# Own double buffer for the sums of w_down, and the convolution's swish split over two stages

## The chip, the cores and the metric

The kernel runs on one core of a Trainium2 chip. The metric is the device time of one execution in microseconds (us), lower is better. A core has a matrix engine (TensorE, in the profile PE, with its weight loads as PEld), VectorE (DVE), ScalarE (ACT), GpSimd (POOL) and SyncE (SP), which here issues the transfers between the main memory and the on-chip memory.

## The reference, cut to what matters

One layer of an encoder over 1024 tokens of width 1024, in float32:

```python
h = rmsnorm(x, norm_mix_pre)
# A) convolution branch: 512 channels
a = a_val * sigmoid(a_gate)                    # columns of h @ w_in
a = silu(layernorm(dwconv31(a), g, b))         # swish is the last step
# B) attention branch: 8 query heads, 2 key/value heads of 64
att = attention(rope(rmsnorm(q)), rope(rmsnorm(k)), v)
x = x + rmsnorm(concat([a, att]) @ w_out, norm_mix_post)
x = x + rmsnorm(cross_attention(rmsnorm(x), mem), norm_mem_post)
u = dwconv3(rmsnorm(x) @ w_up)                 # 2 x 2816 columns
x = x + rmsnorm((gelu(u_gate) * u_val) @ w_down, norm_ffn_post)
```

## The kernel before, in words

Every float32 product is made of three passes: both operands are split into a high part and a low part (`hi = round(v)`, `lo = v - hi`), and `hi*hi + hi*lo + lo*hi` are summed in the matrix accumulator (PSUM). A split is a copy on ScalarE and a subtraction on VectorE or GpSimd.

The stages, in the order of the profile's time: input projection of the convolution branch with its gate and its 31 taps (0 to about 240 us, the taps run on VectorE beside the memory projections); key, value and query projections with their norms and rotations (about 205 to 276); attention (276 to about 500, in 64 units of 128 queries and one head); output projection (480 to 590); cross-attention (590 to 790); the gated MLP's up-projection (780 to about 1250); the down-projection (1250 to the end).

Both MLP products use a recursive scheme with 7 products of blocks instead of 8. For the up-projection, the tokens are split into 4 blocks whose 7 combinations (`BO`, 14 tiles) stay on chip, and a loop over 22 blocks of 128 columns runs one round for each: 7 products of 12 matrix instructions (`product`), the first two in `up_first`, on a weight tile `wg`, the other five in `up_finish`, on combinations that `up_operands` makes of `wg` and `wv`. `up_finish` collects the products on VectorE (`add`, L819), applies the 3-tap convolution (L808, L809, L811), gelu and the multiplication (L842), and stores the result to `act_d` (L843).

The down-projection needs sums of blocks of `w_down`, which don't depend on the data. They are made inside the up-projection's loop, one half block a round: `down_load` fetches 4 blocks of 128x256 into a tile `wd` (L748), `down_sums` does four subtractions in place on VectorE (L754) and stores the tile to `T_d` in the main memory (L755). The down-projection loads them again much later (L892).

On-chip buffers come from pools of slots. A tile that is allocated when no slot is free waits until an older tile of the pool is used up. `raw` has 3 slots of 4 KB and holds the weights as they come from the main memory: in the MLP loop `wg`, `wv` and `wd`. `act` has 15 slots of 8 KB: in the MLP loop the 14 tiles of `BO`, then the tiles `acts` of the down-projection. `wp` has 7 slots of 8 KB: in the MLP loop the split operands `a1`, `a2`, `a3`, `a22` and the tiles `u`; in the query stage the split weights and `n4`, the normed convolution output; in attention the transposed weights `PH`, `PL` of the softmax. `rope` has 2 small slots, which also hold the broadcast reciprocals `rcb` of attention. PSUM has 4 single slots (`psB`) and 2 double ones (`psS`).

The order of the instructions on each engine's queue is set at compile time by a planner: it simulates a timeline and takes, for each engine that is free, the first instruction in program order whose operands and slots are ready. Each engine then runs its list in that order.

The swish of the convolution branch is `conv_apply(h)` for the two halves of the tokens: for each of 4 channel blocks 4 transposes on TensorE, the swish on ScalarE (L381), the high part by VectorE (L382), the low part by GpSimd (L383). Both halves run in attention's second unit (`u == 1`). ScalarE loads a table of functions when it goes from one nonlinear function to another (exp, swish, gelu). In attention the sums of exp are inverted once for two heads (L567), broadcast by GpSimd into `rcb` (L569), transposed on TensorE into `pRb` and multiplied to the output (L571).

Of the kernel before, what the change touches and what calls it, by code (L numbers as in the profile page):

```python
# [8 lines left out]
F32 = mybir.dt.float32  # L9
F32R = mybir.dt.float32r  # L10
AF = mybir.ActivationFunctionType
ALU = mybir.AluOpType
# [5 lines left out]
NF = 22  # L18
# [15 lines left out]
def encoder_block(ctx: ExitStack, tc: tile.TileContext, x, xT, mem, w_a, w_q, w_kv, w_mkv, w_mqT,  # L34
                  w_mo, w_out, w_up, w_down, cols, rows, g10, rope, out):
    nc = tc.nc
# [3 lines left out]
    small = ctx.enter_context(tc.tile_pool(name="small", bufs=4))  # L40
# [6 lines left out]
    def A(shape, name, dt=F32R):  # L47
        return ap.tile([128] + shape, dt, tag="a", name=name)

    def raw(name):  # L50
        return rawp.tile([128, 1024], F32, tag="raw", name=name)
# [4 lines left out]
    def psS(name):  # L56
        return psp.tile([128, 1024], F32, tag="S", name=name, bufs=2)

    def psB(name):
        return psp.tile([128, 512], F32, tag="B", name=name, bufs=4)  # L60

    def sm(n, name, bufs=2):
        return small.tile([128, n], F32, tag=name, name=name, bufs=bufs)

    def f(t):
        return t.bitcast(F32)
# [10 lines left out]
    def cc(i):  # L77
        return col[:, i:i + 1]

    def tr(out_, in_):  # L80
        nc.tensor.transpose(out=out_, in_=in_, identity=ident)  # L81
# [207 lines left out]
    with tc.high_priority(offset=-6000):  # L289
        for c in range(4):  # L290
            a, acc = a_t[c // 2][:, c % 2, :], accs[c % 2]
# [28 lines left out]
    for c in range(8):  # L320
        w = wsplit(w_mqT[c], f"wmq{c}")
        go = tmp("go")
        for g in range(2):
            p = psB("pg")
            for j in range(2):
                for dt_ in range(2):
                    e = (2 * g + j) * 2 + dt_
# [6 lines left out]
    for h in range(4):  # L334
        ws = [wsplit(w_mo[2 * h + j], f"wmo{2 * h + j}") for j in range(2)]
        for mt in range(2):
# [3 lines left out]
            for j in range(2):  # L340
                e = 2 * h + j
# [8 lines left out]
    mxh = [[A([4, 512], f"mxh{h}{g}") for g in range(2)] for h in range(2)]  # L350
    mxl = [[A([4, 512], f"mxl{h}{g}") for g in range(2)] for h in range(2)]
# [3 lines left out]
    def conv_stats(t):  # L355
        h, tt = t // 4, t % 4
        if tt == 0:
            n4[h] = wp.tile([128, 4, 512], F32, tag="w", name="n4")
        p = psS("pln")[:, :512]
        for c in range(4):  # L360
            tr(p[:, c * 128:c * 128 + 128], conv_out[c][:, t * 128:t * 128 + 128])
        n = n4[h][:, tt, :]
        nc.scalar.copy(out=n, in_=p)
        st = sm(6, "ssh2")
        mv = sm(2, "rh2")
        rs = sm(1, "rs")
        nc.vector.bn_stats(out=st, in_=n)
        nc.vector.bn_aggr(out=mv, in_=st)
        rsqrt(rs, mv[:, 1:2], 1, 1.0)
        nc.vector.tensor_scalar(out=n, in0=n, scalar1=mv[:, 0:1], scalar2=rs, op0=ALU.subtract, op1=ALU.mult)  # L370

    def conv_apply(h):
        for c in range(4):
            p = psB("plnT")
            s = n4[h][:, :, c * 128:c * 128 + 128]
            for tt in range(4):
                tr(p[:, tt * 128:tt * 128 + 128], s[:, tt, :])
            p3 = p.rearrange("p (t n) -> p t n", t=4)
            m3 = mxh[h][0][:, c, :].rearrange("p (t n) -> p t n", t=4)
            l3 = mxl[h][0][:, c, :].rearrange("p (t n) -> p t n", t=4)  # L380
            nc.scalar.activation(out=s, in_=p3, func=AF.Silu, scale=cc(C_LNG + c), bias=cc(C_LNB + c))  # L381
            nc.vector.tensor_copy(out=m3, in_=s)  # L382
            nc.gpsimd.tensor_tensor(out=l3, in0=s, in1=f(m3), op=ALU.subtract)  # L383

    b_ctx = tc.issue_after(c_end.ins)
# [57 lines left out]
    bufs, kpair = {}, [None]  # L443
# [50 lines left out]
    for i in range(16):  # L494
        if i < 16:
            (kv_proj if i < 8 else q_proj)(i % 8)
        if i >= 8:
            conv_stats(i - 8)
        upto = min(i - KV_LAG, 7) if i < 8 else min(7, 7 - KV_LAG + 2 * (i - 7))
        while nkv[0] <= upto:  # L500
            kv_transpose(nkv[0])
            nkv[0] += 1
        if i >= 8 + B_LAG:
            q_transpose(i - 8 - B_LAG)
# [4 lines left out]
    att_p, att_t, att_r, att_o = {}, {}, {}, {}  # L509

    def att_unit(u):
        hd, i, qp = (u // 2) % 8, u % 2, u // 16
        return hd, i, qp, qp // 2, (qp % 2) * 256
# [33 lines left out]
    def att_values(v):  # L547
        hd, _, qp, h, q0 = att_unit(2 * v)
        e, pr, kv = hd % 2, hd // 2, hd // 4
        hr = slice(64 * e, 64 * e + 64)  # L550
        PH, PL = att_t.pop(v)
        po = psB("po")[:, :256]
        nc.tensor.matmul(out=po, lhsT=V[:, kv, 0, :], rhs=PH[:, 0, :], start=True, stop=False)
        for k in range(8):
            nc.tensor.matmul(out=po[:64], lhsT=V[:, kv, k, 0:64], rhs=PL[:, k, :], start=False, stop=False)
        for k in range(1, 8):
            nc.tensor.matmul(out=po, lhsT=V[:, kv, k, :], rhs=PH[:, k, :], start=False, stop=k == 7)
        if hd == 0:
            att_o[qp] = tmp("o4")
        o = att_o[qp][:, pr * 256:pr * 256 + 256]  # L560
        nc.scalar.copy(out=o[hr], in_=po[64:128])
        nc.vector.tensor_tensor(out=o[hr], in0=po[:64], in1=o[hr], op=ALU.add)
        if e == 1:
            pb = psB("pRb")
            for i in range(2):
                rc = sm(2, "rc")
                nc.vector.reciprocal(out=rc, in_=att_r[qp, i][:, hd - 1:hd + 1])  # L567
                rcb = small.tile([128, 2, 64], F32, tag="rope", name="rcb", bufs=2)
                nc.gpsimd.tensor_copy(out=rcb, in_=rc.unsqueeze(2).to_broadcast([128, 2, 64]))  # L569
                tr(pb[:, i * 128:i * 128 + 128], rcb.rearrange("p a b -> p (a b)"))  # L570
            nc.vector.tensor_tensor(out=o, in0=o, in1=pb[:, :256], op=ALU.mult)  # L571
            qs_ = slice(q0, q0 + 256)
            nc.scalar.copy(out=mxh[h][1][:, pr, qs_], in_=o)
            nc.gpsimd.tensor_tensor(out=mxl[h][1][:, pr, qs_], in0=o, in1=f(mxh[h][1][:, pr, qs_]), op=ALU.subtract)

    LOOKAHEAD = 3
    for u in range(NU + LOOKAHEAD + 2):
        if u < NU:
            ex = att_scores(u)
            last_exp = ex  # L580
        w = u - LOOKAHEAD
        if 0 <= w < NU:
            att_transpose(w)
        v = w - 2
        if v >= 0 and v % 2 == 1:
            att_values(v // 2)
        if u in (2, 4, 6):
            q_transpose(8 - B_LAG + u // 2 - 1)
        if u == 1:
            conv_apply(0)  # L590
            conv_apply(1)


    def load8(src, name, nact):
# [25 lines left out]
    def transpose_split(src, dh, dl, tt):  # L620
        ts_ = slice(tt * 128, tt * 128 + 128)
        for g in range(2):
            p = psB("pTs")
            for k in range(4):
                tr(p[:, k * 128:k * 128 + 128], src[:, (4 * g + k) * 128:(4 * g + k + 1) * 128])
            p3 = p.rearrange("p (k t) -> p k t", k=4)
            nc.scalar.copy(out=dh[g][:, :, ts_], in_=p3)
            nc.vector.tensor_tensor(out=dl[g][:, :, ts_], in0=p3, in1=f(dh[g][:, :, ts_]), op=ALU.subtract)
# [11 lines left out]
    for t in range(8):  # L640
        h, tt = t // 4, t % 4
        y = psS("y1")
        tok_gemm(y, mxh[h], mxl[h], wo, tt)
        xr = gE[:, 1, :]
        nc.sync.dma_start(out=xr, in_=x[t])
        x1 = post_norm(y, gE[:, 0, :], xr, "x1")
        nc.sync.dma_start(out=x1_d[t], in_=x1)
        j = tmp("junk2")
        ss = sm(1, "ss")
        nc.scalar.activation(out=j, in_=x1, func=AF.Square, accum_out=ss)  # L650
        rsqrt(rs2[:, t:t + 1], ss, 1, 1.0 / D)
        transpose_split(x1, x1h[h], x1l[h], tt)
    rs2s = rstd1

    Gw = load8(G_d, "Gw", 1)
    Ph, Pl = halves("P")
    for t in range(8):
        h, tt = t // 4, t % 4
# [9 lines left out]
        sums, rc = sm(4, "rh8"), sm(4, "ssh2")  # L668
# [72 lines left out]

    T_d = drp.tile([NF // 2, 128, 4, 512], F32, name="T_d")

    wds = {}

    def down_load(fi):
        wds[fi] = raw("wd").rearrange("p (b n) -> p b n", b=4)
        nc.sync.dma_start(out=wds[fi], in_=w_down[fi // 2, :, :, fi % 2 * 256:fi % 2 * 256 + 256])  # L748

    def down_sums(fi):  # L750
        wd = wds.pop(fi)
        b11, b12, b22, b21 = [wd[:, b, :] for b in range(4)]
        for dst, in0, in1 in ((b11, b12, b11), (b12, b22, b12), (b22, b22, b11), (b21, b22, b21)):
            nc.vector.tensor_tensor(out=dst, in0=in0, in1=in1, op=ALU.subtract)  # L754
        nc.sync.dma_start(out=T_d[fi // 2, :, :, fi % 2 * 256:fi % 2 * 256 + 256], in_=wd)  # L755

    def a_split(dst, src, eng):
        nc.scalar.copy(out=dst[:, 0, :], in_=src)  # L758
# [96 lines left out]
    for fi in range(NF + 1):  # L855
        if fi < NF:
            if fi >= UP_PRE:
                up_first(fi)
            up_operands(fi)
            down_load(fi)  # L860
        if fi:
            up_finish(fi - 1)
        if fi < NF:
            down_sums(fi)

# [205 lines left out]
```

## Time and profile before

| | before |
|---|---|
| median of 3 runs | 1469.17 us (1468.13 to 1473.19) |
| profiled execution, its own time | 1470.58 us |
| its span, first to last instruction | 1468.5 us |
| TensorE busy, mean granted clock | 1391.3 us (95%), 0.982 |
| VectorE busy | 1083.4 us (74%) |
| ScalarE busy | 699.1 us (48%) |
| GpSimd busy | 522.3 us (36%) |
| moved by DMA | 170.08 MB |

The time around the span is 2.1 us in the profiled execution. A share of busy time is a mean over stages of different kinds; a stall of TensorE counts where it happens, and after some of them the granted clock is lower for a while.

### The profile page before, as it was taken

What the parts mean: (1) busy time and instruction counts of PE and PEld (TensorE: products, weight loads), DVE (VectorE), ACT (ScalarE), POOL (GpSimd) and SP (SyncE); (2) the same over time, 40 slices, a digit from 0 to 9 for tenths busy, and PEclk for the clock granted to TensorE, in tenths of its full rate; (3) what the DMA queues carried; (4) which work ended last, traced back from release to release, by engine and by line L of the source; (5) the groups of instructions that cost most, each with busy time, mean ns of one, the idle gap of its engine ahead of it and who ended that gap; (6) DMA issues with size and microseconds to landing.
All of it is one profiled execution on the core that took longest, in us unless ns stands there. A gap on an engine that the chain in (4) does not pass through costs nothing.

```text
span 1468.5 us, 18850 instructions
## 1 busy us (share of the span) xinstructions
PE 1391.3 (95%) x7020; PEld 1168.7 (80%) x7020; DVE 1083.4 (74%) x1464; ACT 699.1 (48%) x1192; POOL 522.3 (36%) x508
## 2 busy tenths in 40 slices
PE   7999999889999999999997899999998999999996
PEld 5889988678988888888885677777787777888885
DVE  7599898899999534335468777777777678986576
ACT  6325653678888524334344433343344333544452
POOL 6628877711111414002136533444455441000003
PEclk9999999999999999999998999999999999999999
DMA  6416760000000424113222443343343348622325
GB/s 209 136 50 207 254 240 13 20 1 1 1 2 29 165 94 142 46 43 130 86 86 75 155 143 129 125 135 129 131 129 113 130 143 308 251 90 90 108 86 208
DMA packets 74059, 170.08 MB, mean 116 GB/s; under 512 B 9712, under 2 KB 32496, under 8 KB 73968
## 3 DMA queue, kind: packets, MB, share of 16 engines
q1 hardware_dynamic: 73968, 168.88, 34.2%
q8 instruction: 55, 0.90, 0.3%
q14 instruction: 36, 0.29, 0.1%
HBM read 124.82 MB, written 44.04 MB: 115 GB/s over the span
## 4 chain that ended last, share of the span: by engine, by line
PE 48%; DVE 20%; DMA 12%; issue 8%; POOL 7%; ACT 4%; SPq 1%; DVEq 0%; POOLq 0%; ACTq 0%
DMA wd<-in_w_down_dram 5%; PE yd L91 4%; PE yd L92 4%; PE yd L90 4%; PE y L98 4%; PE y L100 4%; PE y L97 4%; DVE wd L754 3%; PE pPT L81 3%; DMA T_d<-wd 2%; PE sc L100 2%; PE sc L97 2%; PE sc L98 2%; DVE u L819 2%; PE sp L524 2%
## 5 line engine op out<-in xcount | busy, mean ns | idle before, releaser
L295 DVE SCALAR_TENSOR_TENSOR cacc<-conv,col,cacc 128x1009 f32<-128x1009 f32 (+14 forms) x120 | 145.8, 1274 | 4.7 <-ACT cacc L242 4.4
L85 POOL TENSOR_SCALAR rt<-ss 128x1 f32<-128x1 f32 (+1 forms) x43 | 14.9, 347 | 367.6 <-DVE ss L899 228.3
L91 PE MATMUL yd<-op 128*128 128x512 f32 x308 | 119.9, 390 | 0.5 <-DVE op L899 0.5
L92 PE MATMUL yd<-op 128*128 128x512 f32 x308 | 119.7, 389 | 0.0
L758 ACT CAST a<-s 128x512 fp32r<-128x512 f32 x88 | 51.5, 619 | 114.4 <-PE p L100 53.8
L754 DVE TENSOR_TENSOR wd<-wd 128x256 f32<-128x256 f32 x88 | 63.8, 725 | 55.0 <-DMA wd<-in_w_down_dram 40.8
L759 POOL TENSOR_TENSOR a<-wg,a 128x512 fp32r<-128x512 f32 x44 | 61.0, 1406 | 102.5 <-ACT a L758 102.1
L90 PE MATMUL yd<-op 128*128 128x512 f32 x308 | 97.1, 389 | 0.0
L909 ACT CAST op<-acts 128x512 fp32r<-128x512 f32 x77 | 47.9, 622 | 97.7 <-PE yd L92 86.6
L899 DVE TENSOR_TENSOR op<-acts,op 128x512 fp32r<-128x512 f32 x77 | 52.9, 687 | 45.5 <-ACT op L909 45.4
L545 DVE TENSOR_TENSOR PL<-pPT,PH 128x512 fp32r<-128x512 f32 x128 | 82.7, 680 | 5.0 <-ACT PH L544 4.6
L527 DVE TENSOR_REDUCE nm<-sp 128x1 f32<-128x1024 f32 x64 | 78.0, 1219 | 3.2 <-PE sp L525 2.2
L809 DVE SCALAR_TENSOR_TENSOR c<-u,col,c 128x1023 f32<-128x1023 f32 x44 | 56.5, 1284 | 28.9 <-ACT c L808 28.9
L530 ACT ACTIVATE P<-sp,nm 128x1024 f32<-128x1024 f32 x64 | 72.2, 1129 | 8.8 <-PE pPT L81 5.1
L544 ACT CAST PH<-pPT 128x512 fp32r<-128x512 f32 x128 | 69.2, 593 | 13.5 <-PE pPT L81 12.8
L81 PE MATMUL pPT<-ident,P 128*128 128x128 f32 x512 | 69.5, 276 | 2.4 <-DVE PL L545 1.0
L759 DVE TENSOR_TENSOR a<-s,a 128x512 fp32r<-128x512 f32 x88 | 59.4, 694 | 12.3 <-ACT a L758 12.3
L91 PEld LDWEIGHTS yd<-op 128*128 128x128 f32 x308 | 57.8, 188 | 13.2 <-DVE op L899 1.3
L81 PEld LDWEIGHTS pPT<-ident,P 128*128 128x128 f32 x512 | 59.7, 142 | 10.6 <-DVE PL L545 3.1
L90 PEld LDWEIGHTS yd<-op 128*128 128x128 f32 x308 | 57.8, 188 | 12.0
L92 PEld LDWEIGHTS yd<-op 128*128 128x128 f32 x308 | 57.8, 188 | 12.0
L808 ACT ACTIVATE c<-u,col 128x1024 f32<-128x1024 f32 x44 | 53.2, 1209 | 26.9 <-DVE u L819 25.9
(341 smaller groups left out, 4401.0 us busy)
## 6 DMA issues: line engine op xcount, KB each, us to landing
wg<-in_w_up_dram SPq DMA_DIRECT2D x22, 512.0 KB, 3.7
wv<-in_w_up_dram SPq DMA_DIRECT2D x22, 512.0 KB, 4.3
wd<-in_w_down_dram SPq DMA_DIRECT2D x22, 512.0 KB, 3.9
T_d<-wd SPq DMA_DIRECT2D x22, 512.0 KB, 3.2
act_d<-u SPq DMA_DIRECT2D x22, 512.0 KB, 5.1
acts<-act_d SPq DMA_DIRECT2D x22, 512.0 KB, 8.3
st<-T_d SPq DMA_DIRECT2D x20, 512.0 KB, 3.7
wmkv_r<-in_w_mkv_dram SPq DMA_DIRECT2D x16, 512.0 KB, 4.2
```

What stands on the lines that cost most here:

```text
L81: nc.tensor.transpose(out=out_, in_=in_, identity=ident)
L90: nc.tensor.matmul(out=ps, lhsT=sh, rhs=mh, start=first, stop=False)
L91: nc.tensor.matmul(out=ps, lhsT=sh, rhs=ml, start=False, stop=False)
L92: nc.tensor.matmul(out=ps, lhsT=sl, rhs=mh, start=False, stop=last)
L97: nc.tensor.matmul(out=p, lhsT=sh, rhs=mh, start=first, stop=False)
L98: nc.tensor.matmul(out=p, lhsT=sh, rhs=ml, start=False, stop=False)
L100: ins = nc.tensor.matmul(out=p, lhsT=sl, rhs=mh, start=False, stop=last)
L295: nc.vector.scalar_tensor_tensor(out=acc[:, t0:t1_], in0=a[:, t0 + o:t1_ + o], scalar=cc(C_DW + c * 31 + j), in1=acc[:, t0:t1_], op0=ALU.m ...
L527: nc.vector.reduce_max(out=nm, in_=sp, axis=AX.X, negate=True)
L545: nc.vector.tensor_tensor(out=PL[dst], in0=p3, in1=f(PH[dst]), op=ALU.subtract)
L754: nc.vector.tensor_tensor(out=dst, in0=in0, in1=in1, op=ALU.subtract)
L759: eng.tensor_tensor(out=dst[:, 1, :], in0=src, in1=f(dst[:, 0, :]), op=ALU.subtract)
```

## The change

Three edits. First, `wd` leaves the `raw` slots: a tile `wd_b` of two halves is taken once from the `act` pool, a round's load goes into one half a round ahead of its sums, and its store is issued a round behind them. Second, `conv_apply(0)` moves from attention's start into the query stage (`i == 13` of 16), `conv_apply(1)` behind the first token block of the output projection, and the high part goes from VectorE to GpSimd in both. Third, attention inverts its sums for four heads at a time: half as many reciprocals (of 4 columns), as many broadcasts and transposes, half as many multiplications, copies and subtractions of twice the width.

```diff
@@ conv_apply
             nc.scalar.activation(out=s, in_=p3, func=AF.Silu, scale=cc(C_LNG + c), bias=cc(C_LNB + c))
-            nc.vector.tensor_copy(out=m3, in_=s)
+            nc.gpsimd.tensor_copy(out=m3, in_=s)
             nc.gpsimd.tensor_tensor(out=l3, in0=s, in1=f(m3), op=ALU.subtract)
@@ query stage
         if i >= 8:
             conv_stats(i - 8)
+        if i == 13:
+            conv_apply(0)
@@ att_values
-        if e == 1:
+        if hd % 4 == 3:
             pb = psB("pRb")
             for i in range(2):
-                rc = sm(2, "rc")
-                nc.vector.reciprocal(out=rc, in_=att_r[qp, i][:, hd - 1:hd + 1])
-                rcb = small.tile([128, 2, 64], F32, tag="rope", name="rcb", bufs=2)
-                nc.gpsimd.tensor_copy(out=rcb, in_=rc.unsqueeze(2).to_broadcast([128, 2, 64]))
-                tr(pb[:, i * 128:i * 128 + 128], rcb.rearrange("p a b -> p (a b)"))
-            nc.vector.tensor_tensor(out=o, in0=o, in1=pb[:, :256], op=ALU.mult)
-            qs_ = slice(q0, q0 + 256)
-            nc.scalar.copy(out=mxh[h][1][:, pr, qs_], in_=o)
-            nc.gpsimd.tensor_tensor(out=mxl[h][1][:, pr, qs_], in0=o, in1=f(mxh[h][1][:, pr, qs_]), op=ALU.subtract)
+                rc = sm(4, "rc")
+                nc.vector.reciprocal(out=rc, in_=att_r[qp, i][:, hd - 3:hd + 1])
+                for c in range(2):
+                    rcb = small.tile([128, 2, 64], F32, tag="rope", name="rcb", bufs=2)
+                    nc.gpsimd.tensor_copy(out=rcb, in_=rc[:, 2 * c:2 * c + 2].unsqueeze(2).to_broadcast([128, 2, 64]))
+                    tr(pb[:, c * 256 + i * 128:c * 256 + i * 128 + 128], rcb.rearrange("p a b -> p (a b)"))
+            o2 = att_o[qp][:, pr * 256 - 256:pr * 256 + 256]
+            nc.vector.tensor_tensor(out=o2, in0=o2, in1=pb, op=ALU.mult)
+            o3 = o2.rearrange("p (c q) -> p c q", c=2)
+            dst = (slice(None), slice(pr - 1, pr + 1), slice(q0, q0 + 256))
+            nc.scalar.copy(out=mxh[h][1][dst], in_=o3)
+            nc.gpsimd.tensor_tensor(out=mxl[h][1][dst], in0=o3, in1=f(mxh[h][1][dst]), op=ALU.subtract)
@@ attention loop
-        if u == 1:
-            conv_apply(0)
-            conv_apply(1)
@@ output projection
         transpose_split(x1, x1h[h], x1l[h], tt)
+        if t == 0:
+            conv_apply(1)
@@ MLP
-    wds = {}
+    wd_b = A([2, 4, 256], "wd", F32)
+
+    def down_slice(dr, fi):
+        return dr[fi // 2, :, :, fi % 2 * 256:fi % 2 * 256 + 256]
 
     def down_load(fi):
-        wds[fi] = raw("wd").rearrange("p (b n) -> p b n", b=4)
-        nc.sync.dma_start(out=wds[fi], in_=w_down[fi // 2, :, :, fi % 2 * 256:fi % 2 * 256 + 256])
+        nc.sync.dma_start(out=wd_b[:, fi % 2], in_=down_slice(w_down, fi))
 
     def down_sums(fi):
-        wd = wds.pop(fi)
-        b11, b12, b22, b21 = [wd[:, b, :] for b in range(4)]
+        b11, b12, b22, b21 = [wd_b[:, fi % 2, b, :] for b in range(4)]
         for dst, in0, in1 in ((b11, b12, b11), (b12, b22, b12), (b22, b22, b11), (b21, b22, b21)):
             nc.vector.tensor_tensor(out=dst, in0=in0, in1=in1, op=ALU.subtract)
-        nc.sync.dma_start(out=T_d[fi // 2, :, :, fi % 2 * 256:fi % 2 * 256 + 256], in_=wd)
+
+    def down_store(fi):
+        nc.sync.dma_start(out=down_slice(T_d, fi), in_=wd_b[:, fi % 2])
@@ MLP loop
             up_operands(fi)
-            down_load(fi)
-        if fi:
+        if fi == 0:
+            down_load(0)
+        else:
+            down_store(fi - 1)
             up_finish(fi - 1)
         if fi < NF:
             down_sums(fi)
+        if fi + 1 < NF:
+            down_load(fi + 1)
```

## Rows read from the trace of the kernel before

**Rows 1.** Windows by stage: TensorE, weight loads, VectorE, ScalarE, GpSimd, granted clock, DMA
```profile
276.00:320.00 44.00, 32.88 (x189) 26.83 (x188) 41.05 (x58) 35.56 (x58) 19.17 (x23) 0.88 0.00 1
353.00:376.00 23.00, 22.75 (x165) 20.49 (x164) 21.70 (x35) 19.21 (x39) 2.50 (x6) 1.00 0.01 2
500.00:600.00 100.00, 100.00 (x475) 83.47 (x474) 40.41 (x43) 36.86 (x65) 27.30 (x45) 1.00 0.37 125
799.00:1233.00 434.00, 405.96 (x1727) 329.23 (x1727) 326.12 (x420) 163.88 (x227) 194.11 (x146) 0.98 0.42 139
```

**Rows 2.** TensorE's waits, 800 to 1200 us: releaser, total, times, longest
```profile
PE p L97 <- DVE q L819: 16.7, 8, 3.0
PE p L97 <- ACT a L758: 4.4, 2, 2.9
PE p L97 <- DVE u L819: 3.6, 2, 3.1
```

**Rows 3.** Line L842, once a round: duration min/median/max, first and last start
```profile
L842 DVE TENSOR_TENSOR u<-u,c x22: 1206/1210/1222, 822.6 to 1266.2; 128x1024 f32<-128x1024 f32 x22
```

**Rows 4.** TensorE in order of time: the product `t2` of two rounds
```profile
1054.31 0.39 PE L97 MATMUL p<-t2h,a 128*128 128x512 f32 x1
...
1073.35 0.39 PE L97 MATMUL p<-t2h,a 128*128 128x512 f32 x1
```

**Rows 5.** One stall in order of time, SyncE, VectorE, then TensorE
```profile
999.80 0.57 SPq L748 DMA_DIRECT2D wd<-in_w_down_dram  x1
...
1000.50 1.29 DVE L809 SCALAR_TENSOR_TENSOR c<-u,col,c 128x1023 f32<-128x1023 f32 x1 [1.28 <-ACT c L808]
1003.57 1.54 DVE L754 TENSOR_TENSOR wd<-wd 128x256 f32<-128x256 f32 x1 [1.78 <-DMA wd<-in_w_down_dram]
1005.03 0.68 DVE L819 TENSOR_TENSOR q<-p,q 128x512 f32<-128x512 f32 x1
...
1005.85 0.47 PE L97 MATMUL p<-b21h,a 128*128 128x512 f32 x1 [3.00 <-DVE q L819]
```

**Rows 6.** Waits of VectorE, SyncE's queue and ScalarE, 800 to 1200 us
```profile
DVE wd L754 <- DMA wd<-in_w_down_dram: 40.8, 15, 5.0
DVE c L809 <- ACT c L808: 25.6, 25, 1.3
...
SPq L617 <- DMA T_d<-wd: 48.8, 18, 4.4
...
ACT a L758 <- DMA act_d<-u: 77.7, 16, 8.2
```

**Rows 7.** Lines L754, L382 and L569: duration ns min/median/max
```profile
L754 DVE TENSOR_TENSOR wd<-wd x88: 406/424/1539, 798.8 to 1215.8; 128x256 f32<-128x256 f32 x88
...
L382 DVE CAST mxh<-n x8: 415/952/1508, 284.7 to 294.7; 128x512 fp32r<-128x512 f32 x8
...
L569 POOL COPY rcb<-rc x32: 288/293/1293, 298.9 to 481.4; 128x128 f32<-128x128 f32 x32
```

**Rows 8.** A window without a wait of TensorE
```profile
1052.00:1087.00 35.00, 35.00 (x155) 28.95 (x154) 26.24 (x34) 13.63 (x20) 15.33 (x12) 0.99 0.50 165
```

**Rows 9.** TensorE's longest wait, 276 to 320 us, and ScalarE's groups, 276 to 300
```profile
PE sp L524 <- ACT P L530: 7.4, 3, 4.0
...
L381 ACT ACTIVATE n<-plnT,col 128x512 f32<-128x512 f32 x8 | 5.7, 782 | 0.1
L381 ACT ACT_TABLE_LOAD x2 | 2.6, 1283 | 0.0
L530 ACT ACT_TABLE_LOAD x2 | 2.6, 1283 | 2.1 <-DVE nm L527 2.1
```

**Rows 10.** A window at the end of the query stage; eight transposes in the chain of waits
```profile
270.00:276.00 6.00, 6.00 (x32) 5.06 (x31) 5.42 (x10) 3.14 (x6) 4.77 (x9) 1.00 0.28 98
...
708.44 0.87 PE pTs L81 x8
```

**Rows 11.** The page's DMA issues, the stores of the sums: count, KB each, median us to landing
```profile
T_d<-wd SPq DMA_DIRECT2D x22, 512.0 KB, 3.2
```

## The prediction

> **What bounds the kernel now.** I read the windows by stage first. In the output projection TensorE is busy for all of 100 us, in attention for 22.75 of 23.00 us; in the MLP loop it is busy for 406.0 of 434.0 us at a granted clock of 0.98, and over the 44 us in which attention starts for 32.9 at a clock of 0.88 [rows 1]. So there are two places where TensorE loses time, and the reader should see that no other engine is full there, save VectorE at attention's start (41.05 of 44).
>
> How much is lost in the loop follows from its period. The multiplication that ends a round starts 22 times between 822.6 and 1266.2 us, which is 443.6 / 21 = 21.12 us a round [rows 3]. Where TensorE doesn't wait, the same product of two rounds in a row starts 1073.35 - 1054.31 = 19.04 us apart [rows 4]. The excess is 2.08 us a round, 43.7 us in 21 rounds.
>
> Who takes it: TensorE waits 16.7 + 3.6 us for VectorE's sums of products and 4.4 us for ScalarE's splits between 800 and 1200 us [rows 2]. The stall of 3.00 us before 1005.85 shows why VectorE is late: it has a subtraction of the w_down sums at the head of its list, and its tile was only issued at 999.80 and is released at 1003.57; the collection of a product (`q`) runs behind it at 1005.03, and TensorE goes on 0.82 us later [rows 5]. Over the 400 us VectorE waits 40.8 us for `wd`, 15 times. The queue shows the ring behind it: the next weight tile's load waits 18 times, 48.8 us in all, for the store of the sums to land [rows 6]. Three tiles a round pass through three slots, and the slowest to return is `wd`.
>
> **Part 1, the double buffer.** It removes `wd` from the ring of three, and puts the load a round ahead of the sums. Loads, sums and stores are the same 22 each; nothing is added on any engine. VectorE's 40.8 us of waiting then have no cause in the load.
>
> What TensorE gets of this: without the wait the subtraction starts when L809 ends, at 1000.50 + 1.29 = 1001.79; it takes 0.42 us alone, or 1.54 as here [rows 5, 7], so `q` starts at 1002.2 to 1003.3 instead of 1005.03 and TensorE goes on at 1003.0 to 1004.1 instead of 1005.85. That gives back 1.7 to 2.85 of the 3.00 us; I take 2.3, or 77%. TensorE is idle 434.0 - 406.0 = 28.0 us over the loop [rows 1]; less the 4.4 us for ScalarE, 23.6 us are VectorE's, of which 23%, 5.4 us, stay. Of the 4.4 us I keep half, 2.2, because that ring is eased too (two tiles a round in three slots), but the loop's start is also crowded by other splits. The clock, 0.98 over 434 us, is worth some 9 us; it falls after waits, so it stays in their proportion: 9 x 7.6 / 28.0 = 2.4. Idle time and clock explain 37 of the 43.7; of the other 6.7 I keep half, 3.4. So 5.4 + 2.2 + 2.4 + 3.4 = 13.4 us stay and **30 us** go. Bounds: 0 (another wait ends at the same time) and 43.7.
>
> Can the others follow at 19.04 us? In a stretch of 35 us without a wait VectorE is busy for 26.24, which is 14.3 us a round, ScalarE for 7.4 and GpSimd for 8.3 [rows 8]. VectorE also waits 25.6 us in some 19 rounds, 1.3 us a round, for ScalarE's start of the convolution [rows 6]. That makes 15.6, so 3.4 us are free.
>
> What is late next: the tile `u` returns to `wp` when `act_d` has landed, and ScalarE waits 77.7 us for that, 16 times [rows 6]; TensorE waited for ScalarE only in the 4.4 us above. The slot of `wd_b` is the 15th of `act`, which only the raw blocks leave free when the last of the 14 operands is made; the first load can so come late by one landing, some 3.8 us by [rows 5], once. I put it at 0: VectorE is collecting the first products meanwhile; without that cover it costs the 3.8. The tiles `acts` lose that slot until the loop's end, when four operand tiles of the finished first products come free.
>
> **Part 2, the swish.** Attention's start loses 44.0 - 32.9 = 11.1 us of TensorE, and 7.4 of them are three waits for a slot that exp must free [rows 1, 9]. ScalarE is held there by 8 swishes (5.7 us) and four table loads (2 x 2.6 us) that change between swish and exp [rows 9]. Afterwards one load for exp is left there, and the swishes are gone: 5.7 + 3 x 1.28 = 9.5 us less. VectorE loses 8 casts of 0.95 us, 7.6 us [rows 7], from its 41.05. It was the fuller one, so it sets the bound: 41.05 - 7.6 = 33.4, and with its old idle time of 2.95 the stretch is 36.4 instead of 44: 7.6 us gained. The swishes' 32 transposes move to where TensorE is full [rows 1, 10]: 4 x 0.87 = 3.5 us. Net **4 us**.
>
> The moved work's own price: GpSimd gets 4 casts and 4 subtractions near the end of the query stage, where it is busy for 4.77 of 6 us [rows 10]. A cast of 128x512 on GpSimd isn't in the trace; the nearest rows are 0.29 us for a 128x128 broadcast there and 0.42 for the cast on VectorE [rows 7], so 0.4 to 4 x 0.29 = 1.2 us; I take 1.0. Queued behind them are the last queries' norms, for which VectorE and attention's last transposes of the queries wait; they are needed units later, so 0, and 4 x 1.2 = 4.7 us if that cover is gone. In the output projection GpSimd is busy for 27 of 100 us and ScalarE for 37 [rows 1], and the second half's result is read four blocks later: 0, or one table load of 1.3 us. `n4` of the second half now holds a `wp` slot through attention: six are left, three pairs of `PH`, `PL`, and six for the output weights; 0, or one more 128x1024 copy and subtraction in the open, an estimated 2.4 us from L842's 1.21 [rows 3]. Bounds of part 2: from 8 gained to 8 lost.
>
> **Part 3, the reciprocals.** VectorE saves some of its small instructions, but TensorE is busy for 22.75 of 23.00 us in that stretch [rows 1], so of 8 groups at most 8 x 0.25 = 2 us are to be had. Against it, four broadcasts now pass through two slots at a time; the second two wait for TensorE's first transposes. If TensorE has nothing else then, a group costs two broadcasts, 0.6 us, at the most the longest one seen, 1.29 [rows 7]: 5 to 10 us. Other units' transposes are ready in the steady state, so I take 0.
>
> **Sum.** 30 + 4 = 34 us off the profiled execution's own 1470.6 gives 1436.6. That execution lies 1.4 us above the median of 1469.2, so the forecast is **1435**.
>
> **A rule against it.** The subtractions of L754 take 0.42 us in the median and up to 1.54, the casts of L382 0.42 to 1.51 [rows 7]. If each of the four of a round met GpSimd, VectorE would need 14.3 + 4 x (1.54 - 0.42) = 18.8 us, with its 1.3 us of waits 20.1: it would be the bound, the gain 21 x (21.12 - 20.1) = 21 us, and with part 2 the time 1444. The Trainium skill, "SBUF — State Buffer", "Who interferes with whom", says that a VectorE instruction with two on-chip inputs and a GpSimd one that reads the on-chip memory lock each other out for a whole instruction; the spread of these rows agrees.
>
> **Rivals.**
> - *The slots of `wp` take over.* ScalarE's 77.7 us of waiting for `act_d` become TensorE's wait every other round. For it: 16 waits of up to 8.2 us. Against: hardly any reached TensorE. At half of the 30 us the time is 1450.
> - *VectorE is the bound* by the lock above: 1444. Against: the median of 0.42 says that most don't meet.
> - *No change.* The collections are late for other reasons and VectorE idles elsewhere: only part 2 moves, 1465 to 1469. Against: the order of [rows 5].
> - *Slower: SyncE's queue.* The load of round fi + 1 must wait until the store of fi - 1 has left the same half. If that store is issued just ahead, the queue stands for its landing of 3.2 us [rows 11] and 0.6 us of issue [rows 5], and the weight loads behind it are late. From 2.08 us a round on it costs more than is gained; at 3.8 us a round takes 22.8, 36 us more over 21, and the time is 1501. For it: 18 such waits now. Against: the sums are done a round before, so the store can have landed long ago.
>
> **Chances.** Forecast 0.62, `wp` 0.17, VectorE 0.05, all of the 43.7 us and more 0.04, no change 0.05, slower 0.07. A measurement tells 0.3% (4.4 us) from nothing; faster is 0.88, same 0.05, slower 0.07. The range reaches from 1418 (43.7 + 8 gained) to 1462 (a quarter of the 30 us gained, part 2 at 0), which takes in the first two rivals and leaves out the last two.
>
> **What would show it.** Right: no wait of L754 for `in_w_down`; L842 every 19.2 to 19.9 us; TensorE's idle time in the loop under 12 us; the granted clock there at 0.99; two table loads fewer between 276 and 300 us. Part 2 right: L382 on GpSimd in the query stage and behind 500 us, attention's first 20 units some 7 us shorter. Wrong: a new releaser of TensorE in the loop, a weight load that waits for `T_d`, a query stage longer than before by more than 2 us, or transposes of `pRb` with waits for GpSimd.

## The result, and the profile after

The kernel after takes 1455.9 us (median of 6 runs, 1452.9 to 1460.8) beside 1470.4 for the kernel before on the same chip: a ratio of 0.990, 95% interval 0.988 to 0.992. It is 14.5 us faster where 34 were forecast. The profiled execution, 1460.75 us, is the slowest of the six. One of the six executions of the kernel before took 4892.3 us; without it their median is 1470.3.

The windows by stage of the kernel after (columns as in [rows 1]), with the loop cut in two:

```profile
276.00:320.00 44.00, 35.96 (x197) 29.76 (x196) 37.41 (x53) 28.63 (x50) 16.73 (x25) 0.92 0.04 13
799.00:990.00 191.00, 170.51 (x697) 135.79 (x696) 158.06 (x223) 67.36 (x95) 84.19 (x63) 0.95 0.60 198
990.00:1220.00 230.00, 230.00 (x1017) 190.44 (x1015) 167.49 (x197) 95.48 (x131) 111.52 (x84) 1.00 0.29 94
799.00:1233.00 434.00, 413.51 (x1769) 337.00 (x1768) 336.99 (x435) 168.43 (x232) 195.71 (x146) 0.98 0.45 148
```

In the second half of the loop TensorE is never idle. The whole of the 20.5 us of idle TensorE lies in the first 191 us, at a granted clock of 0.95 and with the DMA engines busy for 0.60 of the time. The lines say why (the subtractions of the sums, formerly L754, the multiplication that ends a round, formerly L842, and the cast L382):

```profile
L759 DVE TENSOR_TENSOR wd<-wd x88: 408/418/1522, 807.4 to 969.2; 128x256 f32<-128x256 f32 x88
```
```profile
L849 DVE TENSOR_TENSOR u<-u,c x22: 1207/1211/1222, 822.9 to 1255.1; 128x1024 f32<-128x1024 f32 x22
```
```profile
L382 POOL CAST mxh<-n x8: 607/613/617, 274.1 to 520.7; 128x512 fp32r<-128x512 f32 x8
```

All 88 subtractions now run between 807.4 and 969.2 us, where they had been spread to 1215.8 [rows 7]; the rounds after that have none. A load "a round ahead" in program order may go as soon as its half is free, and the planner let it: loads, sums and stores of 22 rounds were pressed into the first 8 or so. A round takes (1255.1 - 822.9) / 21 = 20.58 us instead of 21.12 [rows 3], so the loop gained 443.6 - 432.2 = 11.4 us.

The waits between 800 and 1200 us, which answer to [rows 2, 6]:

```profile
DVE wd L759 <- DMA wd<-in_w_down_dram: 19.4, 12, 3.5
...
PE p L97 <- ACT a L765: 13.3, 4, 5.0
...
PE p L97 <- DVE u L826: 3.4, 2, 1.8
PE p L97 <- DVE q L826: 2.7, 5, 0.7
```
```profile
SPq L754 <- DMA T_d<-wd: 51.0, 18, 5.5
...
SPq L762 <- DVE wd L759: 35.6, 13, 8.9
```

TensorE's wait for VectorE's collections fell from 20.3 to 6.1 us, but its wait for ScalarE's splits rose from 4.4 to 13.3. SyncE's queue now stands both for the store to land before a load (51.0 us) and for the subtractions before a store (35.6). One stall of the kernel after, in order of time:

```profile
964.12 0.33 SPq L850 DMA_DIRECT2D act_d<-u  x1
...
969.69 0.53 SPq L762 DMA_DIRECT2D T_d<-wd  x1
969.91 1.14 ACT L765 CAST a<-wv 128x512 fp32r<-128x512 f32 x2 [8.48 <-DMA act_d<-u]
...
972.75 0.50 PE L97 MATMUL p<-b11h,a 128*128 128x512 f32 x1 [4.36 <-ACT a L765]
```

ScalarE waits 8.48 us for a slot that the store of `act_d` holds, and that store, issued at 964.12, is put down as what ended the wait at 969.91. TensorE waits 4.36 us for the next tile's split, which ScalarE makes behind this one. Two more of TensorE's four waits for ScalarE are of this form: 4.96 us before 881.56 and 3.06 before 927.41, behind waits of ScalarE of 10.84 and 7.14 us for `act_d`. The three make 12.4 of the 13.3 us.

### The profile page after: what moved, and what is told of

Same layout as the page of the kernel before. It is cut to its first block, busy times and chain, and to the rows that moved or that the text cites. A ratio compares the mean times of both kernels' runs of the same rounds, so it can differ in the third digit from the quotient of the medians.

```text
span 1459.0 us, 18771 instructions
## 1 busy us (share of the span) xinstructions
PE 1388.8 (95%) x7020; PEld 1170.3 (80%) x7020; DVE 1074.9 (74%) x1432; ACT 699.6 (48%) x1184; POOL 523.2 (36%) x508
## 4 chain that ended last, share of the span: by engine, by line
PE 71%; DVE 11%; DMA 9%; issue 3%; ACT 3%; POOL 3%; SPq 0%; POOLq 0%; DVEq 0%; ACTq 0%
PE p L97 6%; PE p L98 6%; PE p L100 6%; PE yd L90 5%; PE yd L91 5%; PE yd L92 5%; PE y L98 4%; PE y L100 4%; PE y L97 4%; DMA wd<-in_w_down_dram 3%; PE pPT L81 3%; DVE wd L759 2%; PE sc L100 2%; PE sc L97 2%; PE sc L98 2%
## 5 line engine op out<-in xcount | busy, mean ns | idle before, releaser
L766 POOL TENSOR_TENSOR a<-wg,a 128x512 fp32r<-128x512 f32 x44 | 62.8, 1448 | 82.4 <-ACT a L765 82.4
L766 DVE TENSOR_TENSOR a<-s,a 128x512 fp32r<-128x512 f32 x88 | 66.7, 772 | 17.2 <-ACT a L765 17.2
L546 ACT CAST PH<-pPT 128x512 fp32r<-128x512 f32 x128 | 69.5, 594 | 13.3 <-PE pPT L81 12.8
L759 DVE TENSOR_TENSOR wd<-wd 128x256 f32<-128x256 f32 x88 | 56.8, 654 | 20.0 <-DMA wd<-in_w_down_dram 19.4
L91 PEld LDWEIGHTS yd<-op 128*128 128x128 f32 x308 | 57.8, 188 | 12.4 <-DVE op L910 0.4
L766 POOL TENSOR_TENSOR a<-wv,a 128x512 fp32r<-128x512 f32 x22 | 33.3, 1533 | 96.0 <-ACT a L765 96.0
```

What stands on the lines that cost most here:

```text
L91: nc.tensor.matmul(out=ps, lhsT=sh, rhs=ml, start=False, stop=False)
L766: eng.tensor_tensor(out=dst[:, 1, :], in0=src, in1=f(dst[:, 0, :]), op=ALU.subtract)
```

## The experiments

"Paced" below is the kernel after with this edit: the load of round fi + 1 is issued no earlier than `act_st[fi - 1]`, the store of `act_d` of round fi - 1. The runs that build on it show their difference from it.

```diff
-            down_load(fi + 1)
+            with tc.issue_after(act_st[fi - 1].ins):
+                down_load(fi + 1)
```

**1. The paced order (`paced`).**

> The changed kernel, with the load of round fi + 1 issued on SyncE only after the store of act_d of round fi - 1, so that loads, sums and stores of w_down go one a round. Theory A (run-ahead: in the changed kernel all 88 subtractions run between 807 and 969 us, in the first 8 of 22 rounds, where rounds take 22.6 us; the other 12 take 19.04): the crowding goes, the loop's rounds after the third take 19.0 to 19.6 us, TensorE's idle time between 799 and 990 us falls from 20.5 to under 10 us, the time is 1433 to 1445 us. Rival B (the loop's first rounds are slow for their own reasons, the splits of the 14 blocks and the slots of wp): the first 8 rounds stay at 22 us and the time stays at 1452 to 1458. Rival C (a load once a round again meets its sums late): VectorE waits for in_w_down as before, the time goes towards 1465.

1455.4 us, ratio 0.9892 (0.9873 to 0.9911): no gain over the kernel after. The heap is gone (the subtractions run from 806.4 to 1229.0 us) and the time is the same, with rounds of 20.52 us spread evenly. So running ahead isn't the cause by itself: theory A fell, and rival B's time came without the slow first rounds that were to cause it. What waits in this kernel between 800 and 1200 us:

```profile
ACT a L765 <- DMA act_d<-u: 69.8, 18, 5.6
...
PE p L97 <- ACT a L765: 8.0, 6, 2.2
PE p L97 <- DVE q L826: 7.2, 9, 1.1
...
DVE wd L759 <- DMA wd<-in_w_down_dram: 1.6, 2, 1.0
...
PE p L97 <- DVE u L826: 1.2, 1, 1.2
```

VectorE hardly waits for the load any more, and TensorE still waits 8.4 us for VectorE and 8.0 for ScalarE.

**2. The parts alone.** `only_db` is the double buffer without the swish and the reciprocals, `only_rest` the other two edits without the double buffer.

> The kernel before with the double buffer of the sums alone; swish and reciprocals as before. By the profiles of before and after the loop gains 9 us and the other parts 5: so A and B both expect 1459 to 1463 us. If the other parts gave nothing or cost, 1454 to 1457.

> The changed kernel with the sums as before (a tile of the ring of three): only the moved swish and the grouped reciprocals are left of the change. My prediction had 4 us of gain: 1465 to 1467. If all of the gain were in the loop: 1469 to 1471.

`only_db` 1461.4 us, 0.9928 (0.9911 to 0.9944), 10.6 us less by the ratio; `only_rest` 1468.6, 0.9981 (0.9964 to 0.9997), 2.8 us by the ratio, between its two expectations. The loop's term was the one that failed.

**3. No sums (`no_sums`).** Loads, subtractions and stores left out; the down-projection reads blocks of `w_down` in their place.

> The changed kernel with the loads, subtractions and stores of the w_down sums left out; the down-projection reads blocks of w_down in their place, so the output is not the reference's. It shows what the sums cost in any order. Theory A: without them all rounds after the third take 19.0 to 19.3 us, and the time is 1430 to 1440, at most 5 us below the paced kernel. Rival B: the first rounds stay at about 22 us, and the time is 1447 to 1455.

1423.0 us in two executions, 0.9665 (0.9643 to 0.9687), below what both theories had. The windows of this run:

```profile
799.00:990.00 191.00, 191.00 (x843) 157.93 (x842) 140.42 (x165) 84.09 (x116) 97.67 (x75) 1.00 0.29 91
990.00:1220.00 230.00, 230.00 (x1017) 190.50 (x1016) 176.23 (x217) 97.87 (x136) 91.79 (x69) 1.00 0.40 137
```

TensorE never waits in these windows, so without the sums no wait is left to remove there. The sums cost some 32 us in the kernel after and in the paced one alike.

**4. Transfers alone, subtractions alone.** `dma_only`: the paced kernel without `down_sums`. `sub_only`: two loads, no stores, and the subtractions queued behind the multiplication (L849) of two rounds before:

```diff
-            down_sums(fi)
+            with tc.issue_after(mult[fi - 2].ins):
+                down_sums(fi)
```

> The paced order with the four subtractions of a round left out; the loads and the stores stay, and the blocks that are stored are the raw ones (so part of the computation is missing). Theory V, VectorE's time for the sums is what the loop pays: without it the round falls to about 19.1 us, TensorE's waits in the loop vanish, and the time is 1425 to 1432. Theory D, the transfers of the sums crowd those of act_d and of the weights and stand in SyncE's queue: the round stays at 20 us or more and the time is 1440 to 1455.

> The paced order with the subtractions alone: 88 as before, a round at a time, on two halves that are loaded once; the other 20 loads and all the stores are left out, and the down-projection reads w_down in their place. Theory V: the round stays at 20 us or more, TensorE still waits for VectorE's collections, 1445 to 1455. Theory D: 1425 to 1432, with a round of about 19.1 us.

`dma_only` 1425.8 us, 0.9683 (0.9662 to 0.9704): paced, all the transfers together cost 2.8 us over no sums. `sub_only` 1433.8, 0.9735 (0.9715 to 0.9754), which neither theory had: VectorE does all 88 subtractions and still 21.5 us of the paced kernel's time are gone. That run differs from the paced one in two things, the transfers and the place in VectorE's list.

**5. The place (`placed`).** The paced kernel with that same edit, all transfers kept; loads a round earlier (`act_st[fi - 2]`).

> The paced order, with one thing moved: the subtractions of round fi are queued on VectorE behind the multiplication that ends round fi - 2 (as in the run with the subtractions alone) and not where GpSimd makes an operand's low part; the loads come a round earlier for it. Transfers, instructions and engines are those of the paced kernel. Theory P, what the sums cost is set by what runs beside them on GpSimd and by what is queued behind them: a subtraction takes 0.45 us in the mean and not 0.82, the round is about 19.2 us and the time 1430 to 1438. Theory T, transfers and subtractions each cost little alone but together stretch the round: 1450 to 1457.

1430.4 us, 0.9715 (0.9699 to 0.9732): 25 us under the paced kernel with the same instructions on the same engines, as theory P had it. With all its transfers it is no slower than `sub_only` (0.9715 and 0.9735, the intervals overlap). VectorE's groups from 990 to 1220 us (busy us, mean ns of one), of the paced kernel and then of this one:

```profile
L766 DVE TENSOR_TENSOR a<-s,a 128x512 fp32r<-128x512 f32 x46 | 38.9, 866 | 17.7 <-ACT a L765 17.7
L759 DVE TENSOR_TENSOR wd<-wd 128x256 f32<-128x256 f32 x44 | 36.2, 822 | 0.8
```
```profile
L766 DVE TENSOR_TENSOR a<-s,a 128x512 fp32r<-128x512 f32 x44 | 39.9, 919 | 3.1 <-ACT a L765 3.1
...
L759 DVE TENSOR_TENSOR wd<-wd 128x256 f32<-128x256 f32 x44 | 18.4, 418 | 0.2
```

A subtraction takes 822 ns in the one place and 418 in the other: 36.2 - 18.4 = 17.8 us over some 11 rounds, 1.6 us a round. The rounds differ by 20.52 - 19.29 = 1.23. What runs beside them is in the paced kernel's order of time, VectorE and then GpSimd:

```profile
1093.61 2.95 DVE L759 TENSOR_TENSOR wd<-wd 128x256 f32<-128x256 f32 x2
1096.48 0.68 DVE L826 TENSOR_TENSOR u<-p,q 128x512 f32<-128x512 f32 x1
1097.08 1.37 DVE L759 TENSOR_TENSOR wd<-wd 128x256 f32<-128x256 f32 x2
```
```profile
1093.10 3.17 POOL L766 TENSOR_TENSOR a<-wg,a 128x512 fp32r<-128x512 f32 x2 [6.81 <-ACT a L765]
1096.24 1.47 POOL L798 TENSOR_TENSOR s<-wv 128x512 f32<-128x512 f32 x1
```

Two subtractions beside GpSimd's two low parts take 2.95 us instead of 0.84, and the collection of a product stands behind them. In the placed kernel they come behind the multiplication, VectorE first (the four start between 1070.80 and 1074.20) and then GpSimd's next work, before which it was idle for 6.13 us. What meets GpSimd there is L766 on VectorE, 1.73 us:

```profile
1069.66 1.22 DVE L849 TENSOR_TENSOR u<-u,c 128x1024 f32<-128x1024 f32 x1
1070.80 0.42 DVE L759 TENSOR_TENSOR wd<-wd 128x256 f32<-128x256 f32 x1
...
1071.73 0.42 DVE L759 TENSOR_TENSOR wd<-wd 128x256 f32<-128x256 f32 x1
...
1075.99 1.73 DVE L766 TENSOR_TENSOR a<-s,a 128x512 fp32r<-128x512 f32 x1
```
```profile
1075.87 2.99 POOL L766 TENSOR_TENSOR a<-wg,a 128x512 fp32r<-128x512 f32 x2 [6.13 <-ACT a L765]
```

**6. The sums on GpSimd (`pool_sums`, `after_pool`, `before_pool`).** One edit on the paced kernel, on the kernel after and on the kernel before:

```diff
-            nc.vector.tensor_tensor(out=dst, in0=in0, in1=in1, op=ALU.subtract)
+            nc.gpsimd.tensor_tensor(out=dst, in0=in0, in1=in1, op=ALU.subtract)
```

> The paced order with the four subtractions of a round on GpSimd in place of VectorE, everything else the same. Theory V: VectorE is free of 1.7 us or more a round, TensorE's waits for VectorE go and the time is 1430 to 1445; what GpSimd's reads cost VectorE beside it keeps it above 1425. Theory D: nothing that matters has moved, 1450 to 1457.

> The kernel after with the four subtractions of a round on GpSimd and nothing else changed; loads and stores run ahead as they like. Theory P: VectorE's list is free of the sums; if they crowd the first rounds on GpSimd, which also makes low parts, these rounds lose some, 1430 to 1445. Theory T: the transfers still come in a heap, 1447 to 1457.

> The kernel before with the four subtractions of a round on GpSimd and nothing else changed: no double buffer, swish and reciprocals as before. Theory P: it is VectorE's list and not the late load that held TensorE, so GpSimd may wait for the load in its place, and nearly all of the loop's loss goes: 1432 to 1442, as much as with the double buffer. If the late load and the ring of three slots are what costs, as the prediction put it: 1460 or more.

`pool_sums` 1430.4 us, 0.9715 (0.9697 to 0.9734); `after_pool` 1444.8, 0.9818 (0.9790 to 0.9847); `before_pool` 1443.0, 0.9792 (0.9770 to 0.9814). The last tells most: with the single tile and its late load, this edit alone takes some 30 us off the kernel before, just above theory P's 1432 to 1442 and far from the 1460 of a loss by the late load. It is as fast as `after_pool` (the intervals overlap): once the sums are on GpSimd, the three edits of the change gain nothing that these runs show. Who waits for the load in `pool_sums` is seen in one line of its waits from 800 to 1200 us:

```profile
POOL wd L759 <- DMA wd<-in_w_down_dram: 130.9, 21, 9.6
```

GpSimd waits 130.9 us for loads, and TensorE is still busy for 396.73 of these 400 us: what stands behind those waits on GpSimd isn't needed soon. And `after_pool` shows what running ahead costs once VectorE's list is clear: 14 us over `pool_sums`, with TensorE busy for 176.89 of the first 191 us and waiting 11.2 us for ScalarE's splits.

**7. The place without the double buffer (`before_placed`).** The second edit of experiment 4 on the kernel before.

> The kernel before with the subtractions of round fi queued on VectorE behind the multiplication that ends round fi - 2, and nothing else changed: one tile of the three slots, its load as before, swish and reciprocals as before. Theory P: place is worth what it was worth on the paced kernel (25 us), so 1443 to 1452; what is then left to the run with the place and the double buffer (1430) is what the late load and the ring really cost, with the 3 us of the swish and the reciprocals. If the late load is the larger part, as the prediction put it: 1460 or more, since VectorE then waits for it in the new place.

1444.7 us, 0.9819 (0.9793 to 0.9846): the place is worth 25 us here too. VectorE's subtractions from 990 to 1220 us, before and with the place:

```profile
L754 DVE TENSOR_TENSOR wd<-wd 128x256 f32<-128x256 f32 x44 | 31.0, 705 | 27.8 <-DMA wd<-in_w_down_dram 19.9 <-DMA act_d<-u 4.1 <-POOL a L759 3.7
```
```profile
L754 DVE TENSOR_TENSOR wd<-wd 128x256 f32<-128x256 f32 x44 | 21.2, 482 | 0.4
```

The wait for the load, 19.9 us of the 27.8 in this window, is gone too, though the tile still comes from the ring of three: in the new place the subtractions come later than the load.

**8. Out of the loop (`early`).** The kernel after with loads, sums and stores moved into the output projection, three rounds behind each token block; `down_round` loads behind the store of that block's `x1`, subtracts and stores.

```diff
@@ output projection
+        for fi in range(3 * t, min(3 * t + 3, NF)):
+            down_round(fi, x1_st)
```

> The kernel after, with loads, sums and stores moved out of the up-projection's loop into the output projection, three rounds behind each token block, where VectorE is busy for 40 of 100 us and the transfers for 0.37. Both theories: the loop runs at 19.05 us a round as it does without the sums. If the output projection has room for them, 1423 to 1432, which beats both kernels; if TensorE comes to wait there for VectorE or for weights, its stage grows by what is left, up to 30 us, and the time goes back to 1455.

1469.0 us, 0.9985 (0.9974 to 0.9997), more than the 1455 that was to be the worst. From 990 to 1220 us TensorE is busy for 229.50 of 230; the gain was lost earlier. Windows of 520 to 600 us and TensorE's longest wait from 480 to 640:

```profile
520.00:560.00 40.00, 38.83 (x183) 31.86 (x182) 22.61 (x41) 11.55 (x23) 10.93 (x23) 1.00 0.93 301
560.00:600.00 40.00, 20.93 (x98) 16.58 (x96) 26.68 (x49) 8.77 (x16) 5.85 (x13) 0.79 0.88 299
```
```profile
PE sc L97 <- ACT Gw L117: 19.7, 1, 19.7
```

SyncE's queue at a load of the sums and at the first of those weights:

```profile
603.47 0.63 SPq L650 DMA_DIRECT2D wd<-in_w_down_dram  x1
607.82 0.33 SPq L115 DMA_DIRECT2D Gw_r<-G_d  x1
```

The transfers are at 0.93 and move 301 GB/s; TensorE waits 19.7 us once for a split of weights of the cross-attention, whose loads stood behind the sums' traffic in SyncE's queue (the split, at 612.29, had waited 18.00 us for its load). VectorE had room there, the transfers did not. So the output projection had no room, and the hope of both theories fell.

The rounds, from the first to the last of the 22 multiplications, beside the times:

| kernel | us a round | time, us |
|---|---|---|
| before, swish and reciprocals alone | 21.41 | 1468.6 |
| before | 21.12 | 1470.4 |
| double buffer alone | 20.68 | 1461.4 |
| after | 20.58 | 1455.9 |
| paced | 20.52 | 1455.4 |
| after, sums on GpSimd | 20.35 | 1444.8 |
| before, sums on GpSimd | 20.10 | 1443.0 |
| before, placed | 19.77 | 1444.7 |
| paced, sums on GpSimd | 19.47 | 1430.4 |
| subtractions alone, placed | 19.46 | 1433.8 |
| paced and placed | 19.29 | 1430.4 |
| no sums | 19.29 | 1423.0 |
| paced, transfers alone | 19.28 | 1425.8 |
| sums in the output projection | 19.16 | 1469.0 |

The rounds are of one profiled execution each. The first two rows have the same code in the loop and differ by 0.29 us a round, 6 us in all, so a difference of that size says nothing by itself.

## Why the prediction was wrong, by its own steps

- **The step that failed** is the loop's 30 us, that is, 13.4 us left over; 11.4 went by the rounds and 10.6 with the double buffer alone. Its parts in the kernel after, between 799 and 1233 us: "Of the 4.4 us I keep half, 2.2" (ScalarE's splits) measured 13.3, because ScalarE came to wait for the slots that `act_d` holds; the clock, of whose 9 us 2.4 were to stay, is still 0.98 over the loop. For VectorE 5.4 us were to stay and 3.4 + 2.7 + 1.0 = 7.1 did. That this one is near is luck: all 7.1 fall before 990 us, in the first eight or so rounds, and the others have no sums.
- **The premise behind it** fails in the paced kernel, which has a round's sums in every round: "without the wait the subtraction starts when L809 ends", with the 77% of a stall that it gave back. The stall was real and the load's lateness ended it in that row, but taking the wait away does not take the subtraction out of its place. It was priced at "0.42 us alone, or 1.54 as here" and the middle taken. In the paced kernel the load is waited for in all for 1.6 us (40.8 before), a subtraction takes 0.82 in the mean from 990 to 1220 us, with a collection behind it, and TensorE waits 8.4 us for VectorE where 5.4 were to stay and 8.0 for ScalarE where 2.2 were; moving the subtractions takes off the 25 us.
- **The rival "The slots of `wp` take over"**, at 0.17 and 1450, is nearest to the kernel after as it ran: TensorE's waits for ScalarE grew from 4.4 to 13.3 us, 12.4 of them behind waits for `act_d`, and the time is 1455.9. The prediction let hardly any of these waits reach TensorE, as in the kernel before.
- **"so 3.4 us are free"**, of VectorE, came from a window picked because TensorE didn't wait in it [rows 8]. That picks the rounds with cheap subtractions: 14.3 us a round there, but 190.31 us busy of the paced kernel's 230, at 20.52 a round, make 17.0. With VectorE's waits for ScalarE (32.1 us for splits and 28.0 for the convolution from 800 to 1200 us, 3.1 a round) 20.1 of the 20.5 are taken. The median of 424 ns [rows 7] hid the same: the mean is 705. But a full VectorE isn't the bound by itself: the same sum for the placed kernel (191.29 us of 230, and waits of 9.0 and 51.6) takes 19.0 of its 19.3, and there TensorE is busy for 230.00 of the 230. What stands behind what on VectorE counts too.
- **The rival "VectorE is the bound"**, at 0.05, was the nearest in mechanism for the paced kernel: 20.1 us a round, where that has 20.5. Its argument against, the median, was the error. The Trainium skill, "SBUF — State Buffer", "Who interferes with whom", has the rule by which a VectorE instruction with two on-chip inputs and a GpSimd one that reads the on-chip memory shut each other out. These runs agree (418 and 822 ns for the same instruction), and the place, which lowers one group to 418, leaves L766 at 919, because that is what meets GpSimd then.
- **"the sums are done a round before, so the store can have landed long ago"** (against the rival of SyncE's queue) was wrong for the kernel after: with the run-ahead the load waits 51.0 us for the store and the store 35.6 for the sums. Nothing in the prediction asked how far ahead the planner would go. By itself this is masked: pacing alone gives 0.5 us, the sums on GpSimd alone 11, both 25.5. Each cause fills the time that the other leaves.
- **The baseline.** 19.04 us a round is the distance of products in the loop's middle; with no sums and no wait the multiplications are still 19.29 apart from first to last. So by that run 443.6 - 405.0 = 38.6 of the 43.7 us were to be had.
- **Part 2 and 3, 4 us net: right in size.** 2.8 us alone (interval 0.4 to 5.3), about 4 between `only_db` and the kernel after by their ratios (0.9928 and 0.990). The shares were others. Attention's scores, first and last start in the kernel after:

```profile
L526 PE MATMUL sp<-KH,Q x128: 389/397/776, 284.6 to 470.1; 128*128 128x512 f32 x128
```

  They span 185.5 us instead of 196.5 (276.5 to 473.0): 11.0 gained by both parts, not 7.6, though TensorE's waits for exp at the start stay (7.6 us in 4, against 7.4 in [rows 9]). The query stage's products got 3.1 us longer, more than the 2 us that the prediction named as a sign of being wrong, and the output projection's 1.9: 5.0 for the moved transposes and what comes with them, not 3.5. With 1.2 us more between the stages the net is 4.8, counted from the query stage on. The profiled execution shows nothing of it where the loop starts (its first product at 768.6 us, 768.5 before), as it had reached the query stage's first product 4.9 us later (230.0, 225.1 before), in stages whose code the change doesn't touch; why isn't known. In `only_rest` that delay is 0.9 us, and the loop's first product starts at 764.5. The cast on GpSimd takes 0.61 us, inside the 0.4 to 1.2 of the estimate. Of the four table loads at attention's start one for exp is left there, and one for swish came to the query stage.
- **What held.** The load's wait itself can be removed (to 1.6 us in the paced kernel; 19.4 are left in the kernel after); parts 2 and 3 paid; the clock went with TensorE's idle time (0.95 where it waits, 1.00 where it doesn't).

The account of the 1455.9 us, from runs: the place is worth 25 us with or without the double buffer (1470.4 to 1444.7, 1455.4 to 1430.4). On the placed kernel the double buffer and pacing with the other two edits are worth 14.3 (1444.7 to 1430.4), of which 3 to 4 are those edits'. `placed` and `pool_sums` are 40 us faster than the kernel before and 25 than the kernel after, by edits of a few lines, and the place alone, with none of the change's three edits, is 11 us faster than the kernel after. Not settled is how the 25 us divide between the longer subtraction and the collection queued behind it; no run kept the one without the other. The remaining 7 us to the run without sums don't come from the rounds, which are as long. The first start of the loop's first product and the multiplications, of the placed kernel and then of the one without sums:

```profile
L97 PE MATMUL p<-b11h,a x88: 387/389/796, 767.8 to 1180.4; 128*128 128x512 f32 x88
L849 DVE TENSOR_TENSOR u<-u,c x22: 1208/1214/1222, 822.1 to 1227.1; 128x1024 f32<-128x1024 f32 x22
```
```profile
L97 PE MATMUL p<-b11h,a x88: 389/389/792, 763.6 to 1169.2; 128*128 128x512 f32 x88
L832 DVE TENSOR_TENSOR u<-u,c x22: 1210/1221/1223, 811.7 to 1216.7; 128x1024 f32<-128x1024 f32 x22
```

From the first product to the first multiplication it is 54.3 us with the sums and 48.1 without. The place is given only to the sums of the third round on; those of the first two still run ahead of the first multiplication, from 807.75 us. With the sums on GpSimd (`pool_sums`) it is 48.9. No run moved those two rounds alone. Another 4.2 us lie ahead of the loop in these two executions, where their code is the same; the placed one is the slowest of its four.

## What to carry to other kernels

Before a wait is credited to the load that ended it, ask what the waiting instruction costs in that place when nothing is late, and what is queued behind it: use the mean and the neighbours on GpSimd, not the median or a stretch picked for being free of stalls. Work that depends on nothing still needs a place and a pace: give a planner that takes whatever is ready a lower bound for both. Time that is free on one engine is not free on the transfer queue.

## What was not expected of the hardware

- Two 128x256 subtractions on VectorE took 2.95 us beside two 128x512 subtractions on GpSimd that themselves took 3.17; apart from those a subtraction takes 0.42.
- The same subtraction on GpSimd, slower by itself (a median of 740 ns), made the kernel 25 us faster than on VectorE in that place:

```profile
L759 POOL TENSOR_TENSOR wd<-wd x88: 714/740/1260, 803.0 to 1192.4; 128x256 f32<-128x256 f32 x88
```

- In `early`, with the DMA engines busy for 0.84 of the time from 500 to 600 us, a 512 KB load of the sums took 6.0 us in the median to land and a store 5.1, beside 3.9 for a load and 3.2 for a store in the kernel before [rows 11].
